# x of a hybrid decoder step turned by VectorE in 32x32 blocks instead of by TensorE, its features grouped as 16 p + k, its norming spread into the input projection's first units

## The chip, the cores and the metric

The kernel runs on one core of a Trainium2 chip. The time is the device time of one execution in microseconds; a kernel's time is the median of its runs. Engines are called TensorE (PE in the profile; PEld are its weight loads), VectorE (DVE), ScalarE (ACT), GpSimd (POOL) and SyncE (SP, which here only issues DMAs).

## The reference, cut to what matters

One layer of a decoder for a prompt of 256 tokens and a sample group of 8 tokens, with D = 2048 features. 264 columns (256 + 8) go through every projection together. The part that the change touches is the norming of x ahead of the input projection, whose matrix w_in is 2048 x 13,856:

```python
def _rmsnorm(x, g):
    xf = x.astype(jnp.float32)
    y = xf * lax.rsqrt(jnp.mean(jnp.square(xf), axis=-1, keepdims=True) + EPS)
    return (y * g.astype(jnp.float32)).astype(x.dtype)

def _in_proj(x, norm_mix, w_in, q_norm_swa, k_norm_swa, q_norm_mem):
    h = _rmsnorm(x, norm_mix)
    q, k, v, z, xbc, dt, qm, g = jnp.split(h @ w_in, _split_points(IN_SPLITS), axis=-1)
...
def _mem_kv(mem, norm_mem, w_mem_kv, k_norm_mem):
    k, v = jnp.split(_rmsnorm(mem, norm_mem) @ w_mem_kv, 2, axis=-1)
    k = _rmsnorm(k.reshape(b, m, MEM_HEADS, MEM_HEAD_DIM), k_norm_mem)
...
def _merge_ffn(x, a_out, s_out, m_out, gates, ...):
    x = x + merged @ w_out
    h = _rmsnorm(x, norm_ffn)
    return x + (jax.nn.silu(h @ w_gate) * (h @ w_up)) @ w_down
```

Behind the projection come window attention, a state-space scan, attention into 256 memory tokens, the merging of the three and a feed-forward part; the change leaves them as they are, but for one reload of x.

## The kernel before, in words

The work of TensorE is a list of units. A unit is one weight load of 512 KB: two blocks of 128 rows by 512 columns. Each weight block is split into a high part (ScalarE, line 181) and a low part (VectorE, line 182), both in a reduced float format, and each product is made of three matmuls: high x high, high x low, low x high. The main loop (the last function printed below, line 1836 and on) takes a unit, issues the loads four units ahead and the splits three units ahead (four raw buffers, three pairs of split buffers), then the unit's matmuls (line 160), then what follows the unit. SP's queue issues nearly all weight loads.

- Units 0 to 31 are the memory projection, in four groups of eight: twelve matmuls a unit, tile pmem. The first two groups give the keys: squares on ScalarE (tile jk, line 446), a reciprocal root in some ten short VectorE instructions (lines 171 to 176), the scaled keys km (line 455), then their transposition on TensorE (kmT). The last two groups give the values vm.
- From unit 32 on stands the input projection, in groups of eight units and four accumulators: 24 matmuls a unit, tile pin. It needs the normed x, turned so that features lie on partitions, split into hh and hl. A partition-block k of 128 features is one of 16; unit 32 + u uses blocks u and u + 8.

All other work is a side task: a generator that is stepped after each unit by about 1 us of work, in a fixed order of tasks (`Side`, lines 36 to 74). A scheduler that simulates the program then puts each engine's instructions in their final order, so that a side task's instructions stand between those of the units.

The norming of x is the task `prep_x` (line 508 on). x comes in four loads of 128 tokens x 1024 features behind the weight loads of units 8 to 11, the sample rows in one load in front of them, all on SP. ScalarE squares them (line 514) and sums along the row; sel and a product with ones spread the sample rows' sums over the partitions; a reciprocal root follows, and a product of ones with a diagonal matrix (dgx, rbx) spreads the prompt's 256 factors over all partitions as rb. Then, for each of the 16 blocks k: two TensorE transpositions of 128 x 128 (xT, lines 546 and 547, helper at 164), a ScalarE copy out of PSUM into xr (line 548), a VectorE multiplication with the gain and rb (xn, line 550), and the split into hh (ScalarE) and hl (VectorE). POOL writes the raw xr to xT_d in DRAM, four blocks at a time (line 553), for the residual sum behind the output projection, which loads it again (line 1657). The gain comes as a 16 x 128 tile and is turned by TensorE with other small vectors (pv).

At unit 30 the main loop drains what is left of `prep_x`. The weights of dt (tile wdt, behind unit 33's load) and the task `dt_work` (xf, pdt) come after it.

Of the kernel before, what the change touches and what calls it, by code (L numbers as in the profile page):

```python
# [8 lines left out]
F32 = mybir.dt.float32  # L9
# [66 lines left out]

# [1 line left out]
def tile_hybrid_decoder_step(  # L78
# [30 lines left out]
    def t4(name, dt=F32):  # L109
        return tp.tile([P, 4 * NT], dt, tag="t4", name=nm(name), bufs=4)  # L110
# [45 lines left out]
    def sps(name):  # L156
        return pq.tile([P, 512], F32, tag="s", name=nm(name))

    def mm(out, lhsT, rhs, start=True, stop=True):
        return nc.tensor.matmul(out, lhsT=lhsT, rhs=rhs, start=start, stop=stop)  # L160

    def tr(out, in_):
        n = in_.shape[0]
        return nc.tensor.transpose(out, in_, ident[0:n, 0:n])
# [14 lines left out]
    def split(hi, lo, src):  # L179

        h = act(hi, src, AF.Copy)  # L181
        return h, V.tensor_tensor(lo, src, hi.bitcast(F32), op=ALU.subtract)  # L182
# [10 lines left out]
    first = {}  # L193
    va = t1("va")[0:96, 0:P]
    vb = t1("vb")[0:59, 0:P]
    vg = [t1("vg")[0:16, 0:P] for _ in range(2)]

    def load_mem(f, n):

# [34 lines left out]
        nc.gpsimd.dma_start(dst, src[0].rearrange("(c p) -> c p", p=P))  # L234
    for h in range(2):
        nc.gpsimd.dma_start(vb[56:57, h * 64:(h + 1) * 64], q_norm_swa)
    nc.gpsimd.dma_start(vg[1], norm_mix[0].rearrange("(c p) -> c p", p=P))
    nc.gpsimd.dma_start(va, conv_w[0].rearrange("k (c p) -> (k c) p", p=P))

    def turn_vectors():  # L240
        p = sps("pv")
        tr(p[:, 64:80], vg[1])
        V.tensor_copy(vgc[:, 16:32], p[:, 64:80])
        tr(p[:, 0:59], vb[0:59])
        tr(p[:, 128:224], va)
        V.tensor_copy(vbc[:, 0:59], p[:, 0:59])
        V.tensor_copy(cw, p[:, 128:224])
# [114 lines left out]
    def w_loads(w, col, nk=KT, first=0):  # L362
        rows = w.rearrange("(k p) n -> p k n", p=P)
# [123 lines left out]

    hh, hl = Feat("hh"), Feat("hl")

    xT_d = dr.tile([P, KT, NT], F32, name="xT_d")  # L490

    x_t = {}

    def load_xs():

        x_t["s"] = t1("xs")[:, 0:P]
        nc.sync.dma_start(x_t["s"], xs_rows.rearrange("b (k n) -> k b n", n=P))

    def load_x_rows(t, h):
        x_t[t, h] = t4("x")[:, 0:1024]  # L500
        nc.sync.dma_start(x_t[t, h], x_prompt[0, t * P:(t + 1) * P, h * 1024:(h + 1) * 1024])

    behind[8] = [load_xs, lambda: load_x_rows(0, 0)]
    for n, (t, h) in ((9, (1, 0)), (10, (0, 1)), (11, (1, 1))):
        behind[n] = [lambda t=t, h=h: load_x_rows(t, h)]

    def prep_x():
        xs = x_t["s"]
        jk = t2("jkx", BF16)
        ss = tiny("ssx", 6)  # L510
        act(jk[:, 0:P], xs, AF.Square, accum_out=ss[:, 4:5])
        for t in range(2):
            for h in range(2):
                act(jk, x_t[t, h], AF.Square, accum_out=ss[:, 2 * t + h:2 * t + h + 1])
            yield 0.5
        sel = tiny("sel", NS)
        V.tensor_reduce(sel, ident.rearrange("p (k b) -> p b k", b=NS), axis=AX.X, op=ALU.add)
        V.tensor_scalar(sel, sel, ss[:, 4:5], None, op0=ALU.mult)
        ps = sps("xn")
        tr(ps[:, 0:P], xs)  # L520
        mm(ps[:, P:P + NS], ones, sel)
        v = tiny("vx", 10)
        V.tensor_tensor(v[:, 0:2], ss[:, 0:4:2], ss[:, 1:4:2], op=ALU.add)
        V.tensor_copy(v[:, 2:10], ps[:, P:P + NS])
        xsT = t1("xsT")[:, 0:P]
        act(xsT, ps[:, 0:P], AF.Copy)
        V.tensor_scalar(v, v, 1.0 / D, EPS, op0=ALU.mult, op1=ALU.add)
        r = rsqrt(v, 10)
        yield 1.5
        dg = t1("dgx")[:, 0:256]  # L530
        for t in range(2):
            V.tensor_scalar(dg[:, t * P:(t + 1) * P], ident, r[:, t:t + 1], None, op0=ALU.mult)
        ps = sps("rbx")
        mm(ps[:, 0:NP], ones, dg)
        rb = t1("rb")
        act(rb[:, 0:NP], ps[:, 0:NP], AF.Copy)
        V.tensor_copy(rb[:, NP:NT], r[:, 2:10])
        yield 0.5
        for q in range(4):
            raw = ev("xr")  # L540
            V.tensor_copy(raw[:, :, NP:NT], xsT[:, 32 * q:32 * q + 32].rearrange("p (c b) -> p c b", b=NS))
            for c in range(4):
                k = 4 * q + c
                h, o = k // 8, (k % 8) * P
                ps = sps("xT")
                for t in range(2):
                    tr(ps[:, t * P:(t + 1) * P], x_t[t, h][:, o:o + P])
                act(raw[:, c, 0:NP], ps[:, 0:NP], AF.Copy)
                tm = t1("xn")
                V.scalar_tensor_tensor(tm, raw[:, c], g_mix[:, k:k + 1], rb, op0=ALU.mult, op1=ALU.mult)  # L550
                split(hh(k), hl(k), tm)
                yield 0.6
            nc.gpsimd.dma_start(xT_d[:, 4 * q:4 * q + 4], raw)


    dt = {}

    def load_dt():

        dt["w"] = t2("wdt")  # L560
        side.ready.add("dtw")
        nc.sync.dma_start(dt["w"].rearrange("p (k n) -> p k n", k=KT),
                          w_in[0, :, C_DT:C_DT + 32].rearrange("(k p) n -> p k n", p=P))

    behind[33] = [load_dt]

    def dt_work():
        ps = sps("pdt")[:, 0:NT]
        for f in range(2):
            full = []  # L570
            for q in (0, 1):
                full.append(ev("xf"))
                h, l = (t.t[f][:, 4 * q:4 * q + 4] for t in (hh, hl))
                V.tensor_tensor(full[q], h.bitcast(F32), l.bitcast(F32), op=ALU.add)
# [1079 lines left out]

    def load_x(i):
        o = t4("xT").rearrange("p (c n) -> p c n", c=4)
        nc.gpsimd.dma_start(o, xT_d[:, 4 * i:4 * i + 4])
# [233 lines left out]
```

## Time and profile before

| | |
|---|---|
| median of three runs | 1866.14 us (1866.09 to 1866.3) |
| the profiled execution | 1865.25 us, its span 1863.5 us |
| TensorE, busy | 1857.1 us, 15126 instructions |
| VectorE, busy | 1196.5 us, 2325 instructions |
| ScalarE, busy | 956.7 us, 1420 instructions |
| GpSimd, busy | 141.3 us, 285 instructions |
| memory read and written | 377.33 MB, 27.81 MB; 217 GB/s over the span |
| first input projection matmul | 106.95 us into the span |

The profile shows one execution. Its chain of waits is followed back from the last instruction: at each step to what released it, or to the instruction before it on its engine. A group row reads: line, engine, operation, out<-in, partitions x elements, count, then busy us and mean ns of one, then the idle time just in front of it. Instructions on one engine overlap, so a mean is longer than the distance from one start to the next.

### The profile page before, as it was taken

To read this page: it belongs to the slowest core of one execution; us is meant where nothing else is said; L and a number is where in the kernel's file an instruction comes from. 1 tells how busy PE (TensorE), PEld (TensorE's weight loads), DVE (VectorE), ACT (ScalarE), POOL (GpSimd) and SP (SyncE) were. 2 spreads that over 40 slices of the span, in tenths; PEclk is the share of its full clock that TensorE was granted. 3 is DMA by queue.
4 is the path that set the end of the run, shared out by engine and by line. 5 is a ranking of instruction groups with operands and counts; after the bars stand their busy time and mean duration, and the time that the engine had idled before them with its cause. 6 is when DMAs were issued, how large, how long until landed. Compare 5 with 4: busy or idle time off the path is not lost.

```text
span 1863.5 us, 37301 instructions
## 1 busy us (share of the span) xinstructions
PE 1857.1 (100%) x15126; PEld 1817.2 (98%) x15126; DVE 1196.5 (64%) x2325; ACT 956.7 (51%) x1420; POOL 141.3 (8%) x285
## 2 busy tenths in 40 slices
PE   9999999999999999999999999999999999999999
PEld 7899999998999999999999999999999999999999
DVE  6765578776788878787465675555445555445565
ACT  6654466656767676664444544444334443334442
POOL 1010001001111111120000001000000000100001
PEclk9999999999999999999999999999999999999999
DMA  8776668667777777887888767556765556865565
GB/s 310 230 238 212 201 228 294 215 219 258 247 223 259 233 249 241 250 257 231 233 229 253 183 198 216 183 187 178 184 185 182 184 184 180 229 209 182 184 189 149
DMA packets 200741, 405.30 MB, mean 217 GB/s; under 512 B 20391, under 2 KB 25494, under 8 KB 200560
## 3 DMA queue, kind: packets, MB, share of 16 engines
q1 hardware_dynamic: 172848, 323.57, 57.5%
q0 software_dynamic: 21552, 74.10, 12.0%
q10 hardware_dynamic: 6168, 5.25, 0.9%
q8 instruction: 118, 1.93, 0.4%
q14 instruction: 55, 0.45, 0.1%
HBM read 377.33 MB, written 27.81 MB: 217 GB/s over the span
## 4 chain that ended last, share of the span: by engine, by line
PE 98%; issue 1%; DMA 0%; DVE 0%; POOL 0%; SPq 0%; POOLq 0%; DVEq 0%
PE pin L160 34%; PE pg L160 14%; PE pu L160 14%; PE pdn L160 13%; PE pout L160 5%; PE pus L160 5%; PE pmem L160 5%; PE pum L160 3%; PE pua L160 2%; PE py L160 1%; PE oms L160 0%; PE pst L160 0%; PE scm L160 0%; PE om L160 0%; PE ps L160 0%
## 5 line engine op out<-in xcount | busy, mean ns | idle before, releaser
L182 DVE TENSOR_TENSOR lo<-raw,hi 128x1024 fp32r<-128x1024 f32 (+1 forms) x651 | 747.1, 1152 | 549.9 <-ACT hi L181 547.9
L181 ACT ACTIVATE hi<-raw 128x1024 fp32r<-128x1024 f32 (+1 forms) x651 | 647.4, 1002 | 824.9 <-PE pin L160 194.1
L160 PE MATMUL pin<-hl,hi 128*128 128x264 f32 x1728 | 486.3, 284 | 0.0
L160 PE MATMUL pin<-hh,hi 128*128 128x264 f32 x1728 | 484.9, 284 | 0.0
L160 PE MATMUL pin<-hh,lo 128*128 128x264 f32 x1728 | 477.2, 284 | 0.0
L160 PEld LDWEIGHTS pin<-hh,hi 128*128 128x128 f32 x1728 | 323.5, 188 | 4.0 <-issue 3.5
L160 PEld LDWEIGHTS pin<-hl,hi 128*128 128x128 f32 x1728 | 324.2, 188 | 2.8 <-issue 2.6
L160 PEld LDWEIGHTS pin<-hh,lo 128*128 128x128 f32 x1728 | 319.3, 188 | 3.1 <-issue 2.9
L160 PE MATMUL pu<-h2l,hi 128*128 128x264 f32 x704 | 197.8, 282 | 0.0
L160 PE MATMUL pu<-h2h,hi 128*128 128x264 f32 x704 | 197.7, 282 | 0.0
L160 PE MATMUL pdn<-fal,hi 128*128 128x264 f32 x704 | 197.7, 282 | 0.0
L160 PE MATMUL pg<-h2l,hi 128*128 128x264 f32 x704 | 197.7, 283 | 0.0
L160 PE MATMUL pdn<-fah,hi 128*128 128x264 f32 x704 | 197.3, 282 | 0.0
L160 PE MATMUL pg<-h2h,hi 128*128 128x264 f32 x704 | 197.0, 282 | 0.0
L160 PE MATMUL pdn<-fah,lo 128*128 128x264 f32 x704 | 194.8, 282 | 0.0
L160 PE MATMUL pu<-h2h,lo 128*128 128x264 f32 x704 | 194.7, 282 | 0.0
L160 PE MATMUL pg<-h2h,lo 128*128 128x264 f32 x704 | 194.4, 282 | 0.0
L160 PEld LDWEIGHTS pdn<-fal,hi 128*128 128x128 f32 x704 | 132.0, 188 | 0.0
L160 PEld LDWEIGHTS pg<-h2l,hi 128*128 128x128 f32 x704 | 132.0, 187 | 0.0
L160 PEld LDWEIGHTS pu<-h2l,hi 128*128 128x128 f32 x704 | 132.0, 187 | 0.0
L160 PEld LDWEIGHTS pg<-h2h,hi 128*128 128x128 f32 x704 | 132.0, 187 | 0.0
L160 PEld LDWEIGHTS pu<-h2h,hi 128*128 128x128 f32 x704 | 131.9, 187 | 0.0
(533 smaller groups left out, 2935.4 us busy)
## 6 DMA issues: line engine op xcount, KB each, us to landing
raw<-in_w_in_dram SPq DMA_DIRECT2D x216, 512.0 KB, 4.4
raw<-in_w_gate_dram SPq DMA_DIRECT2D x88, 512.0 KB, 3.5
raw<-in_w_up_dram SPq DMA_DIRECT2D x88, 512.0 KB, 4.1
raw<-in_w_down_dram SPq DMA_DIRECT2D x88, 512.0 KB, 5.1
raw<-in_w_up_ssd_dram SPq DMA_DIRECT2D x32, 512.0 KB, 5.2
raw<-in_w_out_dram SPq DMA_DIRECT2D x32, 512.0 KB, 5.1
raw<-in_w_mem_kv_dram SPq DMA_DIRECT2D x31, 512.0 KB, 5.6
ring<-in_state_ssm_dram POOLq DMA_DIRECT2D x32, 256.0 KB, 4.1
```

The lines of the kernel that those rows point to most:

```text
L160: return nc.tensor.matmul(out, lhsT=lhsT, rhs=rhs, start=start, stop=stop)
L181: h = act(hi, src, AF.Copy)
L182: return h, V.tensor_tensor(lo, src, hi.bitcast(F32), op=ALU.subtract)
```

## The change

- **x** is loaded with all 128 partitions as (quarter of the features) x (token in a block of 32): eight SP loads of 128 x 512, two behind each of the weight loads of units 8 to 11. VectorE turns it in 32 x 32 blocks: 16 instructions of 128 x 4 x 64, which read with a stride of 16 floats and write rows of 64 neighbouring floats straight into xr. TensorE's 32 transpositions and ScalarE's 16 copies are gone.
- **The features** of block k are then 16 p + k (p the partition) instead of 128 k + p. So all that meets x has to have this order: w_in (a unit's two rows of a partition are neighbours now, 2u and 2u + 1, and partitions lie 16 rows of w_in apart), the weights of dt, the gain (loaded straight as 128 x 16, not turned any more), the sample rows (loaded as 128 x 8 x 16 in pieces of 64 B, by POOL behind the load of conv_w, copied with a stride instead of turned). hh and hl take block k at place k // 2 + 8 (k % 2), so that a unit's matmuls read the places that they read before.
- **The sums of squares** come from eight squares of 512 instead of four of 1024, since a partition holds a quarter of a row; a product with sel adds the quarters. A second product with ones adds up the sample rows'. The root is taken of 16 columns instead of 10.
- **xT_d** lies as 2048 x 264; its reload behind the output projection reads 1056-byte pieces.
- **The draining** of the task is in parts: the first four blocks by unit 30, four more by 32, four more by 34, the rest by 36.

The core of the diff:

```diff
-    def drain(self, name):
+    def drain(self, name, part=None):
-        while any(t[0] == name for t in self.tasks):
+        while any(t[0] == name for t in self.tasks) and part not in self.done:
             g = self._head()
             for _ in g:
-                pass
+                if part in self.done:
+                    return
...
-    nc.gpsimd.dma_start(vg[1], norm_mix[0].rearrange("(c p) -> c p", p=P))
+    nc.gpsimd.dma_start(g_mix, norm_mix[0].rearrange("(p k) -> p k", k=16))
...
-        tr(p[:, 64:80], vg[1])
-        V.tensor_copy(vgc[:, 16:32], p[:, 64:80])
...
+            if order != "(k p) n -> p k n":
+                a, b = 2 * u, 2 * u + 1
...
-        nc.sync.dma_start(x_t["s"], xs_rows.rearrange("b (k n) -> k b n", n=P))
+        nc.gpsimd.dma_start(x_t["s"], xs_rows.rearrange("b (p k) -> p b k", k=KT))
...
+        for b in range(2):
+            nc.sync.dma_start(x_t[j][:, 512 * b:512 * b + 512],
+                              x_prompt[0].rearrange("(b t) (a n) -> b a t n", t=32, a=4)[2 * j + b])
...
+        for b in range(8):
+            act(jk[:, 0:512], x_t[b // 2][:, 512 * (b % 2):512 * (b % 2) + 512], AF.Square, accum_out=ss[:, b:b + 1])
...
-        tr(ps[:, 0:P], xs)
-        mm(ps[:, P:P + NS], ones, sel)
+        mm(ps[0:32, 0:8], sel, ss[:, 0:8])
+        mm(ps[:, 8:16], ones, ss[:, 8:16])
...
-            V.tensor_copy(raw[:, :, NP:NT], xsT[:, 32 * q:32 * q + 32].rearrange("p (c b) -> p c b", b=NS))
+            V.tensor_copy(raw[:, :, NP:NT], xs.rearrange("p b k -> p k b")[:, 4 * q:4 * q + 4])
+            for j in range(4):
+                V.transpose(raw[:, :, 64 * j:64 * j + 64].rearrange("p c (b t) -> p c b t", t=32),
+                            x_t[j].rearrange("p (b f k) -> p k b f", b=2, k=KT)[:, 4 * q:4 * q + 4])
+                yield 0.6
             for c in range(4):
                 k = 4 * q + c
-                h, o = k // 8, (k % 8) * P
-                ps = sps("xT")
-                for t in range(2):
-                    tr(ps[:, t * P:(t + 1) * P], x_t[t, h][:, o:o + P])
-                act(raw[:, c, 0:NP], ps[:, 0:NP], AF.Copy)
                 tm = t1("xn")
                 V.scalar_tensor_tensor(tm, raw[:, c], g_mix[:, k:k + 1], rb, op0=ALU.mult, op1=ALU.mult)
-                split(hh(k), hl(k), tm)
-                yield 0.6
-            nc.gpsimd.dma_start(xT_d[:, 4 * q:4 * q + 4], raw)
+                split(hh(k // 2 + 8 * (k % 2)), hl(k // 2 + 8 * (k % 2)), tm)
+                yield 0.75
+            nc.gpsimd.dma_start(xT_d.rearrange("(p k) n -> p k n", k=KT)[:, 4 * q:4 * q + 4], raw)
+            side.done.add(q)
...
-        group("pin", w_loads(w_in[0], col), KT, hh, hl, after, perm, before, middle)
+        group("pin", w_loads(w_in[0], col, order="(p k) n -> p k n"), KT, hh, hl, after, perm, before, middle)
...
-        if i == 30:
+        if i in (30, 32, 34):
+            side.drain("x", i // 2 - 15)
+        if i == 36:
             side.drain("x")
```

How this moves instructions shows in each engine's order. TensorE of before, where the factors of x are spread (rbx) and the first blocks are turned (xT), between matmuls of the memory projection (pmem):

```order
L160 MATMUL pmem_847<-hi_760,meml_115 128x512
L160 MATMUL pmem_846<-hi_760,memh_113 128x512
L160 MATMUL rbx_574<-dgx_571,ones 128x256
L164 MATMUL xT_599<-ident,x_322 128x128
L164 MATMUL xT_599<-ident,x_377 128x128
L164 MATMUL xT_607<-ident,x_322 128x128
L164 MATMUL xT_607<-ident,x_377 128x128
L160 MATMUL pmem_846<-lo_761,memh_113 128x512
L160 MATMUL pmem_846<-hi_760,meml_115 128x512
```

TensorE of the changed kernel at the same product:

```order
L162 MATMUL pmem_776<-hi_818,meml_115 128x512
L162 MATMUL pmem_777<-hi_818,memh_113 128x512
L162 MATMUL rbx_596<-dgx_594,ones 128x256
L162 MATMUL pmem_777<-lo_819,memh_113 128x512
L162 MATMUL pmem_777<-hi_818,meml_115 128x512
L162 MATMUL pmem_776<-hi_842,memh_113 128x512
L162 MATMUL pmem_776<-lo_843,memh_113 128x512
```

Matmuls of the projection follow at once. From about TensorE's 720th instruction on (some 130 us into the span) the order of every engine is that of before.

VectorE of before, from the split of unit 29 (lo_1176) to that of unit 33 (lo_1257); km is the key norming of the second key group, xn and hl belong to x, xf to dt:

```order
L182 TENSOR_TENSOR lo_1176<-raw_1155,hi_1175 128x2x512
L455 SCALAR_TENSOR_TENSOR km_800<-pmem_507,rs_y_785,knm_bc 128x256 x2
L455 SCALAR_TENSOR_TENSOR km_811<-pmem_508,rs_y_785,knm_bc 128x256 x2
L182 TENSOR_TENSOR lo_1194<-raw_1173,hi_1193 128x512 x2
L182 TENSOR_TENSOR lo_1214<-raw_1191,hi_1213 128x2x512
L550 SCALAR_TENSOR_TENSOR xn_826<-xr_745,vgc,rb_576 128x264
L182 TENSOR_TENSOR lo_1234<-raw_1211,hi_1233 128x1024
L574 TENSOR_TENSOR xf_1250<-hh_121,hl_123 128x1056
L574 TENSOR_TENSOR xf_1252<-hh_121,hl_123 128x1056
L182 TENSOR_TENSOR hl_124<-xn_826,hh_122 128x264
L182 TENSOR_TENSOR lo_1257<-raw_1229,hi_1256 128x1024
```

VectorE of the changed kernel from the end of unit 30's split (lo_1032) to that of unit 31 (lo_1057) and on:

```order
L184 TENSOR_TENSOR lo_1032<-raw_1007,hi_1031 128x512
L553 SCALAR_TENSOR_TENSOR xn_981<-xr_909,vgc,rb_598 128x264
L545 COPY xr_1050<-xs_319 128x4x8
L547 STREAM_TRANSPOSE xr_1050<-x_321 128x4x64
L547 STREAM_TRANSPOSE xr_1050<-x_375 128x4x64
L184 TENSOR_TENSOR hl_122<-xn_977,hh_120 128x264
L176 TENSOR_TENSOR rs_a_728<-rs_y_727 128x4
L553 SCALAR_TENSOR_TENSOR xn_1003<-xr_909,vgc,rb_598 128x264
L184 TENSOR_TENSOR lo_1057<-raw_1029,hi_1056 128x2x512
L547 STREAM_TRANSPOSE xr_1050<-x_406 128x4x64
L547 STREAM_TRANSPOSE xr_1050<-x_437 128x4x64
```

and from the split of unit 32 (lo_1079) to that of unit 34 (lo_1123):

```order
L184 TENSOR_TENSOR lo_1079<-raw_1054,hi_1078 128x1024
L553 SCALAR_TENSOR_TENSOR xn_1094<-xr_1050,vgc,rb_598 128x264
L178 SCALAR_TENSOR_TENSOR rs_y_727<-rs_a_728,rs_y_727 128x4
L184 TENSOR_TENSOR hl_123<-xn_1025,hh_121 128x264
L184 TENSOR_TENSOR lo_1101<-raw_1074,hi_1100 128x1024
L553 SCALAR_TENSOR_TENSOR xn_1116<-xr_1050,vgc,rb_598 128x264
L453 TENSOR_SCALAR rs_y_727<-rs_y_727,rs_m 128x2 x2
L184 TENSOR_TENSOR hl_122<-xn_1094,hh_120 128x264
L457 SCALAR_TENSOR_TENSOR km_742<-pmem_508,rs_y_727,knm_bc 128x256 x2
L457 SCALAR_TENSOR_TENSOR km_753<-pmem_509,rs_y_727,knm_bc 128x256 x2
L184 TENSOR_TENSOR lo_1123<-raw_1098,hi_1122 128x1024
```

The last turning and norming of x (xr_1050 and its xn) now stands between the splits of units 30 to 35, the key norming behind unit 33's instead of ahead of unit 30's, and the kmT transpositions that follow it lie in the projection's first units on TensorE.

More of the change, by code (lines that the diff above doesn't have):

```diff
@@ L41, in __init__ @@
         self.ready = set()
+        self.done = set()
         self.credit = 0.0
@@ L195, in tile_hybrid_decoder_step @@
     vb = t1("vb")[0:59, 0:P]
-    vg = [t1("vg")[0:16, 0:P] for _ in range(2)]
+    vg = [t1("vg")[0:16, 0:P]]
     def load_mem(f, n):
@@ L360, in group, with w_loads @@
                 after=(lambda: after(st["ps"])) if u == nk // 2 - 1 else None))
-    def w_loads(w, col, nk=KT, first=0):
-        rows = w.rearrange("(k p) n -> p k n", p=P)
+    def w_loads(w, col, nk=KT, first=0, order="(k p) n -> p k n"):
+        rows = w.rearrange(order, p=P)
         def f(u):
             a, b = (first + k for k in couples(nk)[u])
+            if order != "(k p) n -> p k n":
+                a, b = 2 * u, 2 * u + 1
             return lambda raw: [(raw.rearrange("p (k n) -> p k n", k=2), rows[:, a:b + 1:b - a, col:col + 512])]
@@ L488, in tile_hybrid_decoder_step, with load_x_rows @@
     hh, hl = Feat("hh"), Feat("hl")
-    xT_d = dr.tile([P, KT, NT], F32, name="xT_d")
+    xT_d = dr.tile([D, NT], F32, name="xT_d")
     x_t = {}
     def load_xs():
-        x_t["s"] = t1("xs")[:, 0:P]
-        nc.sync.dma_start(x_t["s"], xs_rows.rearrange("b (k n) -> k b n", n=P))
[L499 to L505, printed above, removed]
+        x_t["s"] = t1("xs")[:, 0:P].rearrange("p (b k) -> p b k", b=NS)
+        nc.gpsimd.dma_start(x_t["s"], xs_rows.rearrange("b (p k) -> p b k", k=KT))
+    def load_x_rows(j):
+        x_t[j] = t4("x")[:, 0:1024]
+        for b in range(2):
+            nc.sync.dma_start(x_t[j][:, 512 * b:512 * b + 512],
+                              x_prompt[0].rearrange("(b t) (a n) -> b a t n", t=32, a=4)[2 * j + b])
+    behind[8] = [load_xs, lambda: load_x_rows(0)]
+    for j in range(1, 4):
+        behind[8 + j] = [lambda j=j: load_x_rows(j)]
     def prep_x():
@@ L509, in prep_x @@
         jk = t2("jkx", BF16)
-        ss = tiny("ssx", 6)
-        act(jk[:, 0:P], xs, AF.Square, accum_out=ss[:, 4:5])
-        for t in range(2):
[L513 to L518, printed above, removed]
-        ps = sps("xn")
@@ L520, in prep_x @@
-        tr(ps[:, 0:P], xs)
-        mm(ps[:, P:P + NS], ones, sel)
[L522 to L526, printed above, removed]
+        ss = tiny("ssx", 16)
+        sq = t1("xsq")[:, 0:P].rearrange("p (b k) -> p b k", b=NS)
+        act(sq, xs, AF.Square)
+        V.tensor_reduce(ss[:, 8:16], sq, axis=AX.X, op=ALU.add)
+        for b in range(8):
+            act(jk[:, 0:512], x_t[b // 2][:, 512 * (b % 2):512 * (b % 2) + 512], AF.Square, accum_out=ss[:, b:b + 1])
+            if b % 2:
+                yield 0.5
@@ L527, in prep_x @@
+        sel = tiny("sel", 32)
+        V.tensor_reduce(sel, ident.rearrange("p (a t) -> p t a", a=4), axis=AX.X, op=ALU.add)
+        ps = sps("xn")
+        mm(ps[0:32, 0:8], sel, ss[:, 0:8])
+        mm(ps[:, 8:16], ones, ss[:, 8:16])
+        v = tiny("vx", 16)
+        V.memset(v[:, 0:8], 1.0)
+        V.tensor_copy(v[0:32, 0:8], ps[0:32, 0:8])
+        V.tensor_copy(v[:, 8:16], ps[:, 8:16])
         V.tensor_scalar(v, v, 1.0 / D, EPS, op0=ALU.mult, op1=ALU.add)
-        r = rsqrt(v, 10)
+        r = rsqrt(v, 16)
@@ L529, in prep_x @@
         yield 1.5
-        dg = t1("dgx")[:, 0:256]
-        for t in range(2):
-            V.tensor_scalar(dg[:, t * P:(t + 1) * P], ident, r[:, t:t + 1], None, op0=ALU.mult)
+        dg = t1("dgx")[0:32, 0:256]
+        V.tensor_tensor(dg.rearrange("p (b t) -> p b t", t=32), ident[0:32, 0:32].unsqueeze(1).broadcast_to([32, 8, 32]),
+                        r[0:32, 0:8].unsqueeze(2).broadcast_to([32, 8, 32]), op=ALU.mult)
         ps = sps("rbx")
-        mm(ps[:, 0:NP], ones, dg)
+        mm(ps[:, 0:NP], ones[0:32], dg)
@@ L535, in prep_x @@
         rb = t1("rb")
         act(rb[:, 0:NP], ps[:, 0:NP], AF.Copy)
-        V.tensor_copy(rb[:, NP:NT], r[:, 2:10])
+        V.tensor_copy(rb[:, NP:NT], r[:, 8:16])
         yield 0.5
@@ L562, in load_dt @@
         nc.sync.dma_start(dt["w"].rearrange("p (k n) -> p k n", k=KT),
-                          w_in[0, :, C_DT:C_DT + 32].rearrange("(k p) n -> p k n", p=P))
+                          w_in[0, :, C_DT:C_DT + 32].rearrange("(p k) n -> p k n", p=P))
     behind[33] = [load_dt]
@@ L578, in dt_work @@
                 for c in range(4):
-                    k = 8 * f + 4 * q + c
+                    k = 2 * (4 * q + c) + f
                     m = mm(ps[32 * c:32 * c + 32], dt["w"][:, 32 * k:32 * k + 32], full[q][:, c],
@@ L1656, in load_x @@
         o = t4("xT").rearrange("p (c n) -> p c n", c=4)
-        nc.gpsimd.dma_start(o, xT_d[:, 4 * i:4 * i + 4])
+        nc.gpsimd.dma_start(o, xT_d.rearrange("(k p) n -> p k n", p=P)[:, 4 * i:4 * i + 4])
         x2[f"r{i}"] = o
```

1 line of the change is left out of this document (removed).

## The prediction

> **What bounds the kernel now.** I read the page first, then TensorE's waits, then the chain that ended last around the place of the change, then VectorE's timeline there. The page of before:
>
> ```profile
> span 1863.5 us, 37301 instructions
> PE 1857.1 (100%) x15126; PEld 1817.2 (98%) x15126; DVE 1196.5 (64%) x2325; ACT 956.7 (51%) x1420; POOL 141.3 (8%) x285
> ...
> PE 98%; issue 1%; DMA 0%; DVE 0%; POOL 0%; SPq 0%; POOLq 0%; DVEq 0%
> ```
>
> TensorE is busy all through and makes 98% of the chain. Its waits over the whole execution are four, of which these are the largest and the smallest (waited for: us in total, times, longest):
>
> ```profile
> PE idle L160 <- DVE warm L212: 1.5, 1, 1.5
> ...
> PE memT L164 <- DMA ring<-in_mem_prompt_dram: 0.2, 1, 0.2
> ```
>
> So a microsecond of TensorE work taken out is a microsecond off the end, as long as no new wait takes its place. The chain shows what the norming of x costs TensorE (start, us, engine, tile, count):
>
> ```profile
> 22.54 2.76 PE pmem L160 x12
> 25.30 0.16 PE pv L164
> ...
> 52.21 0.11 PE xn L164
> ...
> 53.02 0.12 PE xn L160 x2
> ...
> 66.10 0.44 PE xT L164 x4
> 66.53 4.38 PE pmem L160 x19
> 70.92 0.66 PE xT L164 x6
> ...
> 81.69 17.25 PE pmem L160 x75
> 98.94 0.87 PE kmT L164 x8
> ...
> 108.73 0.44 PE xT L164 x4
> ...
> 112.47 7.12 PE pin L160 x59
> ...
> L164 PE MATMUL xT<-ident,x 128*128 128x128 f32 x32 | 5.0, 272 | 0.0
> ```
>
> Each piece begins where the one before it ends (66.10 + 0.44 = 66.54, and so on): nothing overlaps, nothing waits. A transposition takes 0.11 us of the chain (0.44 / 4), though its own row says 272 ns, since matmuls are pipelined. The chain's nine xT pieces hold all 32. A matmul of the memory projection takes 17.25 / 75 = 0.230 us, a unit of twelve 2.76; one of the input projection 7.12 / 59 = 0.1207, a unit of 24 2.90.
>
> **TensorE: what goes.** Removed: 32 xT transpositions, 32 x 0.11 = 3.52 us; the sample rows' transposition (xn, 52.21), 0.11; the gain vector's (the pv at 25.30), 0.16. Added: the one small product of sel and ones (the two xn at 53.02, one of which is the xs half) becomes two by the order of the changed kernel: one more, taken at 0.12, the whole row, since it is a small product either way. Sum 3.52 + 0.11 + 0.16 - 0.12 = 3.67, rounded to 3.7. Matmuls just behind transpositions run 4.38 / 19 = 0.2305 against 0.230: worth under 0.1 us in all, left in the rounding. From about 130 us on the order of TensorE's instructions is the same in both kernels, so there is no second term of TensorE's.
>
> **ScalarE** loses 16 copies of xT (and the sample rows' copy), and its four squares of 1024 become eight of 512:
>
> ```profile
> L548 ACT ACTIVATE xr<-xT 128x256 f32<-128x256 f32 x16 | 5.5, 383 | 2.2 <-PE xT L164 2.2
> ```
>
> That is 5.5 us of relief on an engine that is not the bound: nothing by itself, but hi parts of the splits no longer queue behind a copy that waits for TensorE (the 2.2 at the end of the row).
>
> **VectorE** gains 16 transpositions of [128 x 4 x 64], and the change puts more of the norming where the projection starts. No row shows such an instruction with a strided source; the nearest are dense ones and a reduction that reads every eighth float, beside a contiguous one of the same length:
>
> ```profile
> L1759 DVE STREAM_TRANSPOSE ring<-yo 128x256 f32<-128x256 f32 x3 | 1.3, 445 | 0.1
> L517 DVE TENSOR_REDUCE sel<-ident 128x8 f32<-128x128 f32 x1 | 0.4, 387 | 0.0
> L1122 DVE TENSOR_REDUCE mxS<-sS 128x1 f32<-128x129 f32 x1 | 0.3, 288 | 0.0
> L176 DVE SCALAR_TENSOR_TENSOR rs_y<-rs_a,rs_y 128x4 f32<-128x4 f32 x6 | 0.9, 158 | 0.1
> ```
>
> Same 256 elements, dense: 445 ns, in a queue of others about 0.37 (the next rows show that neighbours overlap by 0.08). The stride cost the reduction 387 - 288 = 99 ns for 128 elements, so 0.2 for 256: 0.37 to 0.57 us in the queue, 0.45 taken, nearer the dense row because the reduction also writes more. [...] By the upper end the eight transpositions of the tight stretch below cost 1 us more of VectorE and still no wait.
>
> Whether VectorE holds the end is decided where the projection starts. Its timeline of before:
>
> ```profile
> 93.66 1.65 DVE L455 SCALAR_TENSOR_TENSOR km<-pmem,rs_y,knm_bc 128x256 f32<-128x256 f32 x4
> ...
> 103.38 2.42 DVE L574 TENSOR_TENSOR xf<-hh,hl 128x1056 f32<-128x1056 f32 x2
> ...
> 106.06 1.22 DVE L182 TENSOR_TENSOR lo<-raw,hi 128x1024 fp32r<-128x1024 f32 x1
> 107.19 1.30 DVE L550 SCALAR_TENSOR_TENSOR xn<-xr,vgc,rb 128x264 f32<-128x264 f32 x3
> 108.41 1.22 DVE L182 TENSOR_TENSOR lo<-raw,hi 128x1024 fp32r<-128x1024 f32 x1
> 109.54 1.12 DVE L182 TENSOR_TENSOR hl<-xn,hh 128x264 fp32r<-128x264 f32 x3
> 110.57 0.89 DVE L550 SCALAR_TENSOR_TENSOR xn<-xr,vgc,rb 128x264 f32<-128x264 f32 x2
> ```
>
> From start to start: a split's lo 1.13 us, an xn (1.22 / 3) 0.41, an hl (1.03 / 3) 0.34. In the changed order, from the lo of unit 24 to that of unit 36, VectorE has 13 lo (14.7), 14 xn (5.7), 16 hl (5.4), 8 transpositions (3.0 to 4.6), the four km 1.65, one xf 1.2 and some 25 short instructions of 0.13 to 0.16 (row of L176; 3.3 to 4.0): 35.0 to 37.2 us. The time for it: the three split buffers let unit 24's be written when TensorE ends unit 21, and unit 36's must be there when TensorE begins unit 36; between lie ten memory units (27.6), four input units (11.6) and the kmT transpositions (0.87), 40.1 us, less ScalarE's 1.06 for the hi in front (row below), 39.0. Spare: 1.8 to 4.0 us. It fits, narrowly, so I take no wait; each further wait costs what it is long. The key norming (km) of the second key group, ahead of unit 30's lo before, now stands behind unit 33's; it holds two of the five accumulator banks, and the projection's third tile asks for them. With two km and a split ahead of it this is ready some 2 us after the projection's start, and asked for one unit, 2.9, and more after it: hidden by that unit, 0 to 1 us if it isn't.
>
> **Transfers.** All weights, and x, go by SP, the sample rows now by POOL:
>
> ```profile
> 18.27 1.06 ACT L181 ACTIVATE hi<-raw 128x1024 fp32r<-128x1024 f32 x1 [1.48 <-DMA raw<-in_w_mem_kv_dram]
> ...
> q1 hardware_dynamic: 1420, 0.19, 58.7%
> ...
> raw<-in_w_in_dram SPq DMA_DIRECT2D x216, 512.0 KB, 4.4
> ...
> raw<-in_w_mem_kv_dram SPq DMA_DIRECT2D x31, 512.0 KB, 5.6
> ...
> q1 hardware_dynamic: 17847, 30.69, 48.8%
> q0 software_dynamic: 3216, 11.22, 17.1%
> q10 hardware_dynamic: 1376, 1.72, 2.5%
> ...
> L1669 DVE TENSOR_TENSOR x<-pout,xT x16: 423/426/432, 1025.8 to 1097.9; 128x264 f32<-128x264 f32 x16
> L1657 POOL DMA_DIRECT2D xT<-xT_d x4: 528/528/528, 987.8 to 1008.3; - x4
> ...
> DMA to landing us min/median/max: 6.5/9.1/11.3
> ```
>
> - Sample rows in 1024 pieces of 64 B: the 114 to 116 us row (128-byte pieces of dt's weights) gives 58.7% x 16 x 2 us / 1420 = 13 ns a piece on one of 16 engines, 0.85 us over all of them. The first row shows unit 4's split, 2 to 3 us ahead of its use at 22.54, which the 0.85 does not use up. Nothing; 0.85 if that cover is gone.
> - x in eight loads instead of four stands on SP behind units 8 to 11, seven units (19 us) ahead of TensorE: nothing.
> - w_in: a unit's two rows per partition become neighbours, 2 KB pieces as before, but 866 KB apart from partition to partition instead of 54. The five rows behind the first two carry that (landing 4.4 us for w_in, 5.6 for the memory weights; then the shares of the queues from 105 to 300 us). No row shows that distance. Bounds: none, or the second rival below. I take none, since w_mem_kv and w_in, with very different distances, land within 1.2 us of each other.
> - x read again for the output projection, in 512 pieces instead of 128: landed in 6.5 to 11.3 us, the first issued at 987.8 and used at 1025.8, 26 us spare. Nothing.
>
> **The sum.** The profiled execution took 1865.25 us (span 1863.5 and 1.75 around it); less 3.7, 1861.6. The median of the runs is 1866.14, 0.9 above it, so 1866.14 - 3.7 = 1862.4, and with a tenth for the small waits that a tight VectorE leaves: **1862.5**.
>
> **The rivals.**
> A. VectorE comes late where the projection starts. It decides once a strided transposition takes over about 0.8 us (0.57 + 1.8 / 8). For it: the spare of 1.8 us is a sum over a dozen units, and a burst inside can miss one. Against: VectorE is three units ahead there. 0.5 to 3 us of stall: 1863 to 1865.5.
> B. The other side: the strided transposition is a slow form altogether. From 0.57 + (1.8 + 3.7) / 8 = 1.26 us each the gain is gone, from 1.75 the kernel is slower by over 0.2%; at 2 us each, 1862.5 + 8 x 1.2 = about 1872. Against it: the stride cost the reduction 0.8 ns an element, and this would need 6.
> C. Weight rows 866 KB apart load slower. The loading queue's share is 48.8%, the others take about 20%, so it decides from (100 - 20) / 48.8 = 1.64 times the packet time; at twice, 118% of the time, 18% of 216 x 2.9 us: +113, about 1975. [...]
> D. The removed work was not the whole price: a weight stream or side task that follows TensorE's place (x's writes on POOL now go ahead of the key outputs) gives part back, 0.5 to 2 us of gain left: 1864.1 to 1865.6. Against it: no TensorE wait of before names raw.
>
> **How the numbers follow.** Forecast without a new wait (1861.5 to 1863.0) 0.64, A 0.20, D 0.07, B 0.05, C 0.04. A measurement of this kernel can tell about 0.2%, 3.7 us: 1862.4 is the line, and the forecast sits on it, so its 0.64 splits 0.34 faster, 0.30 same. Same: 0.30 + 0.20 + 0.07 = 0.57. Slower: 0.05 + 0.04 = 0.09. The range reaches from the forecast's lower end, 1861.5, over A and D to 1866.0; left out are B and C and what lies below.
>
> **What would show it.** Right: TensorE's busy time down by 3 to 4 us, no xT pieces in the chain, the first pin piece at about 103.1 instead of 106.95 (3.0 us of the removed pieces lie ahead of it, and kmT's 0.87 moves behind it), no TensorE wait over 0.3 us between 60 and 130, transpositions at 0.4 to 0.7 us. Wrong: a TensorE wait for lo or hl between units 28 and 38 (A, B), for raw anywhere behind unit 32 (C), a first pin piece as late as before (D).

## The result and the profile after

| | before | changed |
|---|---|---|
| median | 1866.12 us (1865.4 to 1866.56, 6 runs) | 1880.93 us (1879.85 to 1882.11, 6 runs) |
| ratio | | 1.0079, 95% interval 1.0069 to 1.009 |
| first input projection matmul | 106.95 us | 121.76 us |

The changed kernel is 14.8 us slower, where 3.6 less than before was forecast. The page of the changed kernel:

```profile
span 1880.4 us, 37230 instructions
PE 1861.2 (99%) x15094; PEld 1815.4 (97%) x15094; DVE 1203.0 (64%) x2340; ACT 952.8 (51%) x1410; POOL 142.2 (8%) x286
...
PE 95%; DMA 3%; issue 1%; ACT 0%; DVE 0%; POOL 0%; POOLq 0%; SPq 0%; ACTq 0%; DVEq 0%
```

The chain now holds 3% of DMA, 53 us, where it held 5.4. Not all of that is loss, since the chain is followed along what came last, but its pieces in the first 140 us show where to look (start, us, what):

```profile
28.20 16.99 DMA raw<-in_w_mem_kv_dram
...
45.63 14.75 DMA raw<-in_w_mem_kv_dram
...
62.83 6.89 PE pmem L162 x22
...
79.33 0.48 PE xn L162 x4
...
92.87 0.62 PE rbx L162 x2
93.49 28.27 PE pmem L162 x122
121.76 3.39 PE pin L162 x28
...
135.74 0.58 PE pdt L162 x8
```

The chain spends 17 and 15 us in two weight loads of the memory projection; before, the median of one from issue to landing was 5.6. From 62.83 on TensorE is the chain again. So the loss stands between 37 and 70 us, long before the place that the prediction argued about. TensorE's waits for weights, over the whole execution (us in total, times, longest):

```profile
PE pmem L162 <- ACT hi L183: 9.0, 4, 3.5
...
PE pmem L162 <- DVE lo L184: 1.1, 2, 0.5
```

What stands in front of those weights is x. SP's queue (start, us in the issue, tile, count; an issue of weights alone mostly takes 0.4 us, and I read a much longer one as waiting for room in the queue, which no view shows directly), and the DMA engines from 34 to 42 us:

```profile
29.46 9.46 SPq L504 DMA_DIRECT2D x<-in_x_prompt_dram  x2
39.02 2.46 SPq L260 DMA_DIRECT2D raw<-in_w_mem_kv_dram  x1
41.53 4.01 SPq L504 DMA_DIRECT2D x<-in_x_prompt_dram  x2
45.63 19.32 SPq L260 DMA_DIRECT2D raw<-in_w_mem_kv_dram  x6
```

```profile
DMA  9723231332122232222132222222222232232222
GB/s 225 154 72 92 92 113 61 102 102 102 61 113 92 102 113 82 92 92 113 72 123 82 113 92 92 113 82 113 92 92 113 82 113 92 82 123 82 92 113 82
```

The digits are tenths of 16 DMA engines: for 7 us only two to three tenths are busy, at some 100 GB/s. Four engines of 16 would be 0.25, the other twelve idle while the weights wait; whether it is that is for the experiments.

The waits are not the whole loss. The two kernels' windows (busy us of TensorE, its weight loads, VectorE, ScalarE and GpSimd, each with the number of instructions, then the granted TensorE clock, the DMA share and GB/s) from 45 to 60 us, of before and of the changed kernel:

```profile
45.00:60.00 15.00, 15.00 (x73) 12.41 (x72) 11.01 (x33) 11.55 (x22) 1.64 (x3) 1.00 0.72 248
```

```profile
45.00:60.00 15.00, 10.46 (x24) 6.84 (x24) 4.16 (x14) 4.35 (x11) 0.00 (x0) 0.66 0.63 191
```

24 matmuls instead of 73; and where TensorE does work, its granted clock is 0.66 on average, and those 24 take 10.46 us, 0.44 each. TensorE's timeline of the changed kernel behind the wait that ends at 45.98 shows them 0.43 us apart at first, and 0.23 again from 49.73 on, which is the distance of before:

```profile
46.88 0.63 PE L162 MATMUL pmem<-lo,memh 128*128 128x512 f32 x1
47.31 0.63 PE L162 MATMUL pmem<-hi,meml 128*128 128x512 f32 x1
...
49.73 0.39 PE L162 MATMUL pmem<-hi,meml 128*128 128x512 f32 x1
49.96 0.39 PE L162 MATMUL pmem<-lo,memh 128*128 128x512 f32 x1
```

So the idle time is paid for a second time here, in slow matmuls: some 30 of them between 46 and 67 us, at 0.43 us apart instead of 0.23, cost over 6 us more than at the distance of before.

### The profile page after: what moved, and what is told of

It reads as the page before. It is cut to its first block, busy times and chain, and to the rows that moved or that the text cites. A ratio compares the mean times of both kernels' runs of the same rounds, so it can differ in the third digit from the quotient of the medians.

```text
span 1880.4 us, 37230 instructions
## 1 busy us (share of the span) xinstructions
PE 1861.2 (99%) x15094; PEld 1815.4 (97%) x15094; DVE 1203.0 (64%) x2340; ACT 952.8 (51%) x1410; POOL 142.2 (8%) x286
## 4 chain that ended last, share of the span: by engine, by line
PE 95%; DMA 3%; issue 1%; ACT 0%; DVE 0%; POOL 0%; POOLq 0%; SPq 0%; ACTq 0%; DVEq 0%
PE pin L162 33%; PE pg L162 13%; PE pu L162 13%; PE pdn L162 12%; PE pout L162 5%; PE pus L162 5%; PE pmem L162 3%; PE pum L162 2%; PE pua L162 2%; DMA raw<-in_w_mem_kv_dram 2%; PE py L162 1%; DMA ld<-in_cache_mem_v_dram 0%; PE pst L162 0%; PE oms L162 0%; PE scm L162 0%
```

## The experiments

Theory: the new load of x keeps to four of the 16 DMA engines. Its source steps over the four feature quarters outermost (a, then the 32 tokens), and the weights queued behind it on SP wait for their shares on those four. Rivals: the 2 KB pieces of x load slowly on any engine; SP has more to issue; the sample rows' 64-byte pieces, moved to POOL, hold up the early weights.

### x on 16 engines

```diff
-        for b in range(2):
-            nc.sync.dma_start(x_t[j][:, 512 * b:512 * b + 512],
-                              x_prompt[0].rearrange("(b t) (a n) -> b a t n", t=32, a=4)[2 * j + b])
+        for a in range(4):
+            nc.sync.dma_start(x_t[j][32 * a:32 * a + 32].rearrange("t (b n) -> t b n", b=2),
+                              x_prompt[0].rearrange("(b t) (a n) -> a t b n", t=32, a=4)[a][:, 2 * j:2 * j + 2])
```

> The changed kernel, x loaded in sixteen loads of 32 partitions (one feature quarter, two token blocks) instead of eight of 128 that step over the four quarters outermost; order of all other instructions the same. Theory (four engines): the eight loads run on 4 of the 16 DMA engines at 100 GB/s, and the weights queued behind them on SP wait for their shares on those four; with 32 tokens outermost the loads use all 16, the waits for raw between 37 and 62 us go, the DMA share in that stretch is no longer 0.2 to 0.3, and the TensorE work that was removed shows: 1862 to 1865 us. Rival (pieces): 2 KB pieces out of rows that lie 8 KB apart load slowly on any engine, or the number of issues on SP counts: 1880 us or more, since the pieces are the same and the issues twice as many. Rival (sample rows): the 64-byte pieces on POOL hold the early weights: 1880, no change.

Measured: 1870.63 us (1868.7 to 1873.94, 7 runs), ratio to before 1.0027 (1.0016 to 1.0037). 10.3 of the 14.8 us come back, with the same pieces and twice the issues, so those two rivals fall as the main cause; the sample rows stay on POOL here, so they are not what came back either. But it is still 4.8 us slower than before, which the theory did not expect (1862 to 1865). The window of this run from 25 to 41 us, and the same one of before:

```profile
25.00:41.00 16.00, 15.23 (x70) 11.88 (x70) 8.35 (x24) 8.41 (x20) 0.54 (x1) 1.00 1.05 248
```

```profile
25.00:41.00 16.00, 16.00 (x75) 12.78 (x74) 10.97 (x31) 11.73 (x29) 0.53 (x1) 1.00 1.01 363
```

All 16 engines are busy in both (DMA shares 1.05 and 1.01), but they move 248 GB/s instead of 363. A second thing is slow about this load; it gets runs of its own below. The execution that this profile shows took 1873.94 us, the longest of the seven, and 2.5 us of its waits are for a cache load far behind x (tile oms; 0.3 in the changed kernel's), so its rows stand for the middle run only roughly.

### The kernel before, x on four engines

```diff
-        nc.sync.dma_start(x_t[t, h], x_prompt[0, t * P:(t + 1) * P, h * 1024:(h + 1) * 1024])
+        nc.sync.dma_start(x_t[t, h], x_prompt[0, t * P:(t + 1) * P].rearrange("(t a) d -> a t d", a=4)[:, :, h * 1024:(h + 1) * 1024])
```

> The kernel before, with the rows of x read in four interleaved groups outermost (token 4 t + a at partition 32 a + t, so tokens are permuted and the output with them); nothing else is changed, four loads of 4 KB pieces. Theory (four engines): 2 MB over 4 engines at 100 GB/s take 21 us instead of 5, so the weights come 16 us late less some slack, TensorE cools and loses some more: 1878 to 1888 us, with waits for raw between 35 and 62 us. Rivals (pieces, sample rows): nothing of theirs is in this kernel: 1866 us.

Measured: 1884.18 us (1882.38 to 1885.37, 4 runs), ratio 1.0096 (1.0082 to 1.011). Its TensorE waits for hi:

```profile
PE pmem L160 <- ACT hi L181: 9.1, 4, 4.5
```

Its DMA rows from 30 to 45 us show the stretches of two tenths at about 100 GB/s in this kernel too, and the granted clock, 1.00 before, was 0.71 from 45 to 60 us:

```profile
DMA  7889899974322222222257999932222222222224
GB/s 186 257 208 273 213 229 289 197 164 104 109 93 93 109 98 109 98 98 104 76 153 273 311 268 246 224 77 87 87 109 109 98 104 98 104 93 104 104 104 115
```

```profile
45.00:60.00 15.00, 9.09 (x22) 5.92 (x23) 3.75 (x11) 4.24 (x11) 0.00 (x0) 0.71 0.62 189
```

One line of the old kernel, with 4 KB pieces, four issues and all 128 partitions, gives the loss: 18.4 us. Less the TensorE work that the change removes (3.7 us in the prediction's sum, 2.4 in the run with x in whole tiles below) that makes 14.7 to 16.0, and the changed kernel lost 14.8.

### x on two engines

```diff
-        for b in range(2):
-            nc.sync.dma_start(x_t[j][:, 512 * b:512 * b + 512],
-                              x_prompt[0].rearrange("(b t) (a n) -> b a t n", t=32, a=4)[2 * j + b])
+        for b in range(2):
+            for c in range(2):
+                nc.sync.dma_start(x_t[j][64 * c:64 * c + 64, 512 * b:512 * b + 512],
+                                  x_prompt[0].rearrange("(b t) (a n) -> b a t n", t=32, a=4)[2 * j + b, 2 * c:2 * c + 2])
```

> The changed kernel, each load of x cut into two of 64 partitions that step over two feature quarters outermost: 16 loads on 2 engines. Theory (four engines): the engines that hold x up carry twice as much, 42 us instead of 21 at 50 GB/s, so the loss grows by about 20 us: 1895 to 1907 us, DMA share about 0.13 while x loads. Rivals (pieces, sample rows): the same pieces and bytes, 1881 us; by the number of issues 1883.

Measured: 1901.18 us (1900.1 to 1901.83, 4 runs), 20.3 above the changed kernel. The DMA rows of this run from 40 to 60 us:

```profile
DMA  1111111117996111111111111111111111689721
GB/s 49 45 45 49 49 49 49 49 61 217 319 340 197 49 45 53 45 49 49 49 49 49 49 49 53 49 41 49 49 49 53 66 49 53 135 299 356 279 70 49
```

About half the share of the engines (one tenth against two to three), half the rate (49 GB/s against about 100), and the loss grows by about the 22 us that 2 MB take longer at 49 than at 100 GB/s. I read the bursts between as the other engines' shares of the next weight load. Over the runs the share goes with the number of steps of the load's outermost dimension: two to three tenths at about 100 GB/s with 4, in the changed kernel and in the kernel before with its tokens in four groups; one tenth at 49 GB/s with 2. With 32, 64 and 128 steps (the run on 16 engines, the one with 64 partitions below, and before) the windows from 25 to 41 us have 1.05, 1.03 and 1.01, the weights in them. What picks the engines no run shows.

### x by ScalarE's queue

```diff
-            nc.sync.dma_start(x_t[j][:, 512 * b:512 * b + 512],
+            nc.scalar.dma_start(x_t[j][:, 512 * b:512 * b + 512],
```

> The changed kernel, the same eight loads of x issued by ScalarE's queue instead of SP's. Theory in its narrow form (the weights wait behind x in the queue of each of the four engines): on a queue of their own the loads share the four engines with the weights, which need 12 GB/s of about 25 on each: most of the loss goes, 1863 to 1870 us. Wider form (the four engines' rate is what counts, whatever the queue): about as now, 1876 to 1882 us. Rival (sample rows): 1880 us.

Measured: 1883.26 us (1882.72 to 1885.13, 4 runs). No gain, but the run does not tell the theory's two forms apart: the issues themselves held ScalarE up, before the features of the memory rows (memh) that TensorE needs. ScalarE's timeline:

```profile
18.82 6.43 ACTq L504 DMA_DIRECT2D x<-in_x_prompt_dram  x2
25.30 0.47 ACT L390 ACTIVATE memh<-memT,vgc 128x256 fp32r<-128x256 f32 x1 [9.93 <-issue]
28.64 0.54 ACTq L504 DMA_DIRECT2D x<-in_x_prompt_dram  x1
29.23 0.47 ACT L390 ACTIVATE memh<-memT,vgc 128x256 fp32r<-128x256 f32 x1 [3.45 <-DMA x<-in_x_prompt_dram]
```

Whether four engines shared by two queues would have hidden x is left open.

### Four engines, but spaced

```diff
-    behind[8] = [load_xs, lambda: load_x_rows(0)]
-    for j in range(1, 4):
-        behind[8 + j] = [lambda j=j: load_x_rows(j)]
+    for n in range(8):
+        behind[8 + n] = [lambda n=n: load_x_rows(n // 2, n % 2)]
+    behind[8].insert(0, load_xs)
...
-        if i == 9:
+        if i == 11:
             side.ready.add("go")
```

(each call now issues one load)

> The changed kernel's eight loads on four engines, one behind each of the weight loads of units 8 to 15 instead of two behind 8 to 11. Theory (the backlog of the four engines sets the loss): from about 22 us on, the four engines have 21 us of x and eight weight shares of 1.3 us, 31.5 us of work in 22 us of units, a backlog of 9.6 us instead of 15.3; so about 6 us of the loss go, 1873 to 1878 us, with the DMA share at 0.2 to 0.5 for longer. Rival (the spacing decides, as it does for loads on 16 engines): 1862 to 1867. Rival (each load costs a fixed wait): 1881.

Measured: 1880.08 us (1879.79 to 1882.58, 4 runs): the theory's 1873 to 1878 was a miss. The time is near the last rival's 1881, but no trace shows that rival's reason. The waits for hi did fall, from 9.0 to 4.3 us. TensorE's waits and VectorE's timeline of this run:

```profile
PE pmem L162 <- DVE lo L184: 8.3, 3, 7.2
PE pmem L162 <- ACT hi L183: 4.3, 3, 1.9
```

```profile
70.47 0.17 DVE L641 TENSOR_SCALAR pack<-pack 128x16 f32<-128x16 f32 x1 [10.64 <-DMA pack<-in_swa_sinks_dram]
```

A small constant load (pack), issued by SP behind the weights, came late, and VectorE sat 10.64 us in front of the instruction that needs it, with the next split's lo behind that. From 66 to 70 us the DMA share is 0.27 at 99 GB/s, as while x loads, so I take it that pack stood behind x on the same four engines. By that reading the backlog only moved to another customer of the queue.

### x in whole tiles: what the rest of the change is worth

```diff
-        for b in range(2):
-            nc.sync.dma_start(x_t[j][:, 512 * b:512 * b + 512],
-                              x_prompt[0].rearrange("(b t) (a n) -> b a t n", t=32, a=4)[2 * j + b])
+        t, h = j % 2, j // 2
+        nc.sync.dma_start(x_t[j], x_prompt[0, t * P:(t + 1) * P, h * 1024:(h + 1) * 1024])
```

> The changed kernel, but x loaded as the kernel before loads it: four loads of 128 tokens x 1024 features on all partitions and 16 engines. The data then stand in the wrong places, so the output is not the reference's; all instructions and their order are those of the changed kernel. It shows what the rest of the change is worth. Theory (the load of x is all that went wrong): the removed TensorE work comes back whole, 1861.5 to 1864.5 us, no wait for hi or lo between 30 and 130 us, first input projection matmul near 103. Rival (the transpositions at 0.61 us or the new order make VectorE late as well): 1865 to 1868. Rival (sample rows on POOL): waits before 30 us, 1865 or more.

Measured: 1863.4 us (1862.8 to 1864.19, 11 runs), ratio 0.9987 (0.9978 to 0.9995), 2.4 us below the 1865.8 beside it; no wait for hi or lo at all, first input projection matmul at 103.9. So with x loaded at the old price the change is a gain, as forecast in kind: 2.4 us, and by the interval of the ratio 0.9 to 4.1, so the 3.7 of the sum are not ruled out by the time alone. All engines where the projection starts, in this run and before:

```profile
80.00:120.00 40.00, 40.00 (x243) 35.06 (x242) 38.18 (x86) 24.86 (x46) 6.14 (x12) 1.00 0.87 259
```

```profile
80.00:120.00 40.00, 40.00 (x245) 34.86 (x247) 32.73 (x69) 25.14 (x48) 7.29 (x12) 1.00 0.80 263
```

VectorE is busy for 38.2 of 40 us instead of 32.7, and TensorE still for 40.00.

### The sample rows back on SP

```diff
-        nc.gpsimd.dma_start(x_t["s"], xs_rows.rearrange("b (p k) -> p b k", k=KT))
+        nc.sync.dma_start(x_t["s"], xs_rows.rearrange("b (p k) -> p b k", k=KT))
```

on top of the kernel with x in whole tiles.

> The kernel of the run with x loaded in whole tiles (1863.4 us), the sample rows issued by SP behind unit 8's weights again instead of by POOL at the start; x still in the wrong places, so the output is not the reference's. Theory (the 1024 pieces of 64 B that POOL starts at 6 us take DMA time from the memory rows and weights that TensorE waits for): the memT waits before 20 us fall from 1.2 us to about 0.9, as before the change: 1862.6 to 1863.2 us. Rival (they cost nothing there and 0.85 us of DMA time at 22 us instead): 1863.4 us, or up to a microsecond more.

Measured: 1864.1 us (1863.86 to 1864.96, 11 runs), ratio to before 0.9988 (0.998 to 0.9997), against 0.9987: no gain. The memT waits fell from 1.2 to 0.6 us, and nothing came of it. The sample rows on POOL cost nothing that these runs can see.

### The second price: loads into part of the partitions

The kernel before, x in loads of 32 partitions (and, in a second kernel, of 64 in the same way):

```diff
-        nc.sync.dma_start(x_t[t, h], x_prompt[0, t * P:(t + 1) * P, h * 1024:(h + 1) * 1024])
+        for a in range(4):
+            nc.sync.dma_start(x_t[t, h][32 * a:32 * a + 32], x_prompt[0, t * P + 32 * a:t * P + 32 * a + 32, h * 1024:(h + 1) * 1024])
```

> The kernel before, each load of x cut into four of 32 partitions, 4 KB pieces as before, 16 issues on SP; the output is the reference's. Theory (narrow target): in the run with x on 16 engines the engines were busy all through while x loaded, at 220 to 250 GB/s instead of 380, since a load into 32 partitions has a narrower way into SBUF; here x takes 9 us instead of 5.5, some of it hidden by the seven units of lead: 1867 to 1871 us, DMA share 0.9 or more at 200 to 280 GB/s between 25 and 42 us. Rival (2 KB pieces were the slow part): 4 KB pieces load at the full rate, 1866 us. Rival (SP's number of issues): 1868 us with the DMA share below 0.8 in that stretch.

> The kernel before, each load of x cut into two of 64 partitions (0 to 63, 64 to 127), 4 KB pieces on 16 engines; the output is the reference's. [...] Rival (the rate grows with the number of partitions): about half of the loss, 1867 to 1869 us at 270 to 300 GB/s. Rival (the number of issues on SP was the loss, 16 there and 8 here): 1866 to 1867 us.

Measured: 1871.05 us with 32 (1869.51 to 1873.64, 7 runs; ratio 1.0028, 1.0017 to 1.0038) and 1871.53 with 64 (1868.82 to 1872.56, 11 runs; ratio 1.0025, 1.0017 to 1.0034). Windows from 25 to 41 us, with 32 and with 64:

```profile
25.00:41.00 16.00, 15.48 (x70) 12.03 (x70) 7.99 (x25) 6.98 (x16) 0.53 (x1) 1.00 1.05 228
```

```profile
25.00:41.00 16.00, 15.54 (x71) 12.44 (x72) 9.24 (x29) 8.90 (x20) 0.53 (x1) 1.00 1.03 253
```

The pieces are 4 KB and the engines are all busy (DMA shares 1.05 and 1.03), yet the rate is 228 and 253 GB/s instead of 363; and twice the partitions and half the issues make no difference to the time. So it is neither the size of the pieces nor the number of issues, and the rate does not grow with the number of partitions from 32 to 64 as it would have to for the loss to halve: both rivals of the run with 64 fall. What is left is that loads into 32 or 64 of the 128 partitions are slower; the narrower way into SBUF was the author's guess at the reason, and no view shows a reason.

Then, whether the order of the four quarter loads matters in the changed kernel with x on 16 engines:

```diff
-        for a in range(4):
+        for a in (0, 2, 1, 3):
```

> The changed kernel with x in sixteen loads of 32 partitions, four behind each of units 8 to 11 as in the run with x on 16 engines (1870.6 us), but the four in the order of quarters 0, 2, 1, 3 instead of 0, 1, 2, 3; nothing else differs. [...] Rival (the rate falls with the number of partitions, whichever they are): 1870.6, the same GB/s.

Measured: 1868.0 us (1866.66 to 1872.55, 11 runs), ratio 1.0014 (1.0005 to 1.0023) against 1.0027 for the plain order; 265 GB/s against 248:

```profile
25.00:41.00 16.00, 16.00 (x75) 13.05 (x75) 9.27 (x26) 8.46 (x19) 0.53 (x1) 1.00 1.04 265
```

The two intervals overlap, and the 248 GB/s come from the slowest run of their kernel, so the 2.6 us are likely rather than shown; the direction, less time and more GB/s, is against the rival. Why the order should matter was not shown.

### A version meant for use

```diff
+        for a in (c, c + 2):
+            nc.sync.dma_start(x_t[j][32 * a:32 * a + 32].rearrange("t (b n) -> t b n", b=2),
+                              x_prompt[0].rearrange("(b t) (a n) -> a t b n", t=32, a=4)[a][:, 2 * j:2 * j + 2])
...
+    for n in range(8):
+        behind[8 + n] = [lambda n=n: load_x_rows(n // 2, n % 2)]
...
-        if i == 9:
+        if i == 11:
```

(c is 0 in the first call for a tile and 1 in the second.)

> The changed kernel with x in sixteen loads of 32 partitions on 16 engines, but two behind each of the weight loads of units 8 to 15 (quarters 0 and 2, then 1 and 3) instead of four behind units 8 to 11; the task of x starts two units later for that. Theory: two such loads take about 1.2 us and a weight load 1.3 us of the engines, 2.5 of the unit's 2.76, so weights stay in time: 1862 to 1866 us. Rival (rate is not the matter, the new place is lost elsewhere): 1869 us or more. Rival (the later start of the task makes VectorE late before unit 36): 1866 to 1869 with waits for lo or hl between 85 and 125 us.

Measured: 1865.77 us (1863.74 to 1872.71, 12 runs), ratio 1.0004 (0.9996 to 1.0013): no different from before, at the upper end of the theory's 1862 to 1866, and with a wider spread. Window of this run from 25 to 41 us:

```profile
25.00:41.00 16.00, 16.00 (x74) 12.79 (x74) 10.77 (x29) 10.97 (x24) 0.53 (x1) 1.00 1.04 292
```

TensorE has no wait there, but the engines move 292 GB/s, not 363, and 0.4 us of hi and 0.9 of lo are waited for later, between 55 and 63 us. The 32 x 32 blocks need each feature quarter on 32 partitions of its own, and no load tried here brings that about both on 16 engines and into all 128 partitions at once; whether one could is open. No kernel that puts x where it belongs beat the kernel before.

## Why the prediction was wrong

**The step that failed** is in the part on transfers: "x in eight loads instead of four stands on SP behind units 8 to 11, seven units (19 us) ahead of TensorE: nothing." It priced x's load by its issues and its lead, and took for granted that 2 MB move at the old rate. The runs put in its place: four engines, about 100 GB/s, 2 MB in some 21 us instead of 5.8 (at the 363 GB/s of before), every later load on SP behind it; put into the kernel before, that alone costs 18.4 us. No rival named it either: A, B and D look at VectorE and the projection's start, C at w_in. The lead of seven units was real and was used up: by 37 us both kernels have begun 35 of the 128 products hi x memh. By 62 us, before has begun 70 and the changed kernel 50:

```profile
L160 PE MATMUL pmem<-hi,memh x70: 387/393/776, 8.0 to 61.4; 128*128 128x512 f32 x70
L162 PE MATMUL pmem<-hi,memh x50: 387/396/796, 7.2 to 61.9; 128*128 128x512 f32 x50
```

A product is three matmuls of 0.23 us, so that is 13.8 us; by 70 us it is 80 against 56, 24 products or 16.6 us, and it does not grow further. The waits for hi and lo (10.1 us) and the slow matmuls behind them (over 6) add up to that, and the removed work takes some 2 us off again.

**What should have raised the question** was in the diff: the outermost dimension of the new source has 4 steps, where that of the old one is its 128 tokens. No row of before that the prediction read shows such a load, so by the prediction's own manner its cost should have been bounded from both sides, and the upper bound was open.

**TensorE's removed work**, 3.67 us in the sum, is right in kind: 2.4 us (0.9 to 4.1) with x at the old price. In that run TensorE's busy time fell from 1857.1 to 1855.3 us, 1.8 where 3 to 4 were forecast, and the first input projection matmul came at 103.9 where 103.1 was. The small pieces were undersized. The prediction also read one of the two xn at 53.02 as the sample rows' half; the trace has both as sel and ones, so one product is two instructions. From the chain of the changed kernel, the two small products take 0.48 us (xn x4) where 0.23 stood for the transposition and the product before; the sum had 0.01 for the difference. rbx takes 0.62 instead of 0.43. And the products of dt, which the sum left out, come in four pieces between the projection's matmuls instead of two:

```profile
138.44 0.58 PE pdt L162 x8
...
148.59 0.56 PE pdt L162 x2
...
151.51 1.02 PE pdt L162 x14
```

with the 0.58 at 135.74 that is 2.74 us against 1.48 + 0.58 = 2.06; the run with x in whole tiles has the same four pieces. Together 0.24 + 0.19 + 0.68 = 1.1, and 3.67 - 1.1 = 2.6, against 2.4 measured. The pieces are read from traces; the interval of the time is too wide to confirm a difference of 1.1.

**VectorE** was right in its outcome, wrong in one size. A transposition takes 612 ns, 0.58 in the queue (9.3 us / 16), just above the upper bound of 0.57 and not the 0.45 taken:

```profile
L547 DVE STREAM_TRANSPOSE xr<-x 128x256 f32<-128x256 f32 x16 | 9.3, 612 | 0.0
```

The price of the stride, taken from the reduction (387 against 288 ns), was near: 167 ns more than the dense 445 for 256 elements, where 99 for 128 gave 198. The upper end was the better value. The spare of 1.8 to 4.0 us held: no wait of TensorE's for lo behind unit 28 in the run with x in whole tiles. Rivals A and B did not come about.

**The other transfers** were right: no TensorE wait for raw of w_in (rival C, whose doubled packet time no run shows), none for the reload of x, nothing for the sample rows (one run that moved them back) and nothing for the later key norming. Rival D named a part of the gain given back; by the pieces above about a third was, but by TensorE's own small products and not by a transfer.

## What to carry to other kernels

Before a changed load is called hidden, read its two access patterns: how many steps the outermost dimension has, and how many partitions it writes (in loads of 32 or 64 the kernel before lost some 5 us). A load that is small in bytes can hold the loads behind it if it keeps to few DMA engines, as 2 MB did here for 18.4 us in the kernel before, and the sign in these profiles is a DMA share that stands still, at two to three tenths (about 100 GB/s) or at one tenth (49 GB/s), while something waits for a DMA. A change that saves work on the bounding engine is worth only what the loading of its new layout leaves of it, and that is quickly tried by itself: load the old way, whatever the values, and see what the rest is worth.

## What the runs showed of the hardware

- TensorE's granted clock fell behind long waits: behind those of 3.5 and 2.7 us in the changed kernel it was 0.66 on average from 45 to 60 us, with matmuls 0.43 us apart instead of 0.23; in the run with x on two engines, with waits of 5.6 to 7.2 us, 0.52 from 50 to 60 us (its window):

```profile
50.00:60.00 10.00, 4.65 (x11) 3.68 (x12) 1.45 (x4) 1.72 (x4) 0.00 (x0) 0.52 0.27 95
```

- Shorter waits went either way. In the run with x on 16 engines a wait of 1.72 us that ends at 46.01 left the clock at 1.00; in the one with 32 partitions, a wait of 1.57 us that ends at 42.05 was followed by 0.69. The windows, in this order:

```profile
44.00:48.00 4.00, 1.75 (x7) 0.94 (x6) 1.23 (x1) 3.00 (x8) 0.00 (x0) 1.00 1.06 295
```

```profile
44.00:48.00 4.00, 3.27 (x10) 2.27 (x8) 0.38 (x1) 1.46 (x3) 0.00 (x0) 0.69 1.01 202
```

- Two DMA issues on ScalarE's queue held ScalarE for 6.43 us, while x loaded (its DMA rows from 23 to 32 us stand at two tenths and about 100 GB/s).
- With x loaded into 64 neighbouring partitions at a time the kernel before took as long as with 32: 1871.5 and 1871.1 us, at 253 and 228 GB/s from 25 to 41 us, against 1865.8 to 1866.2 us and 363 GB/s into all 128.
